# Decoder trunk on one core: residual kept by token, output, query and key products with the tokens as the stationary operand

## The chip, the cores and the metric

One core of one Trainium2 chip runs the whole program. The time is the device time of one execution in microseconds (us); the runs of the kernel before lie between 2883.8 and 2883.99.

## The reference

A trunk of two layers works on 256 tokens of 2048 features in float32. Each layer adds three branches to the residual `h`; all its weights are read once per execution.

```python
def reference(x, mem, ...):                      # D_MODEL 2048, SEQ 256, N_MEM 256, D_FF 5632, DEPTH 2
    h = x
    for l in range(DEPTH):
        h = h + hybrid_mixer(rms_norm(h, norm_mix[l]), ..., w_in[l], ..., w_out[l])
        h = h + memory_cross_attention(rms_norm(h, norm_x[l]), rms_norm(mem, norm_mem[l]),
                                       xa_wq[l], xa_wk[l], xa_wv[l], xa_wo[l])
        h = h + conv_ffn(rms_norm(h, norm_ffn[l]), ffn_w_up[l], ffn_conv[l], ffn_conv_b[l], ffn_w_down[l])
    return rms_norm(h, norm_final)

def memory_cross_attention(h, m, wq, wk, wv, wo):   # 4 heads of 512
    q, k, v = (h @ wq), (m @ wk), (m @ wv)          # each split into heads
    p = softmax(einsum('bthd,bmhd->bhtm', q, k) * 512 ** -0.5)
    return einsum('bhtm,bmhd->bthd', p, v) @ wo

def conv_ffn(h, w_up, conv_w, conv_b, w_down):
    g, val = split(causal_dwconv(h @ w_up, conv_w) + conv_b)   # 3 taps along the tokens
    return (silu(g) * val) @ w_down
```

The mixer projects into 4880 columns (linear attention, windowed attention, short convolution) and back with `w_out`.

## The kernel before

**Products.** Every float32 operand is split into a high and a low part (`hi = round(x)`, `lo = x - hi`), and a product is `hi*hi + hi*lo + lo*hi`. Weights come through `stream`: SyncE's queue (SP) loads a tile `raw` of 128 x 1024 (512 KB, 4 buffers), ScalarE (ACT) casts `wh` (line 160), VectorE (DVE) subtracts `wl` (line 161), with 3 buffers each. Two ways of multiplying stand side by side, and both sum in one of two pairs of PSUM banks:

- `wstat` keeps a 128 x 128 block of weights stationary. The result has features on partitions and tokens along the free axis. Its moving operand is the activations: `wh` meets 512 columns (high and low parts of 256 tokens), `wl` meets 256 columns (high parts). A group makes 256 features.
- `xstat` keeps 128 tokens stationary and moves the weights, 512 columns at a time. The result has tokens on partitions. A group makes 512 features.

In this text a **k step** is the work on 128 rows of a weight matrix and 512 of its columns. It takes 8 matmuls in `wstat` (four pairs of 512 and 256 columns) and 6 in `xstat` (all of 512 columns): 3072 columns either way. One `raw` tile holds two k steps.

**Layouts.** Before the change the residual `h` has features on partitions (8 tiles of 2 x 256). `w_fm` (part of the mixer's input), the keys `wk`, the queries `wq`, and the three products back to the residual, `wo`, `wxo` and layer 0's `wd` (tile `res`, `project_residual`), use `wstat`. `wv` (tile `vp`), `w_q`, `w_tok`, the feed-forward `wu` (tile `up`) and layer 1's last product `fin` keep tokens stationary. `up` has to be turned to features on partitions for the convolution: `turn` transposes 32 x 32 blocks on VectorE (line 226), writes the tile to DRAM (`z_d`, line 228, SP) and reads it back with the blocks in place (four DMAs, line 230, SP, which wait for the write). 44 groups of `up` are turned so. `ffn_group` then multiplies the turned tile by the row factors (line 1022).

**Residual.** After each of the eight groups of `res`, VectorE adds it to `h` in two instructions (lines 777 and 778), ScalarE squares it, VectorE sums the squares in `acc`, and `prep` makes the next stage's operand (lines 263 on ScalarE, 264 on VectorE) in place. `row_factor` sums `acc` over partitions with small matmuls (line 314, tile `ss`), takes the inverse root and spreads it over the partitions (line 299, tile `rbp`). In layer 1, `residual_by_token` turns `h` with 32 TensorE transposes (line 792, tile `hT`) during `up`, because `final` needs it by token.

**Order.** The program is written as one main line of products with tasks beside it (generators). Each call of `pump` lets one task run to its next `yield n`, after which it rests `n` calls. A product calls `pump` once or twice per k step, 32 times for 512 features in either form. `W` holds the rests: a turned group's second half waits `up=22` calls. A scheduler orders instructions on each engine from that program; `high_priority` moves some forward, `keep_in_program_order` holds some in place. Each engine and the SP queue run their instructions in order.

**Stages of a layer**, in order: `tokp`, `zkq`, `zq`, `zc`, `zb`, `zr` (mixer input), `kp` (keys), `res` from `wo`, `qp` (queries, with attention scores), `vp` (values), `res` from `wxo`, `up`, then `res` from `wd` (layer 0) or `fin` (layer 1).

Of the kernel before, what the change touches and what calls it, by code (L numbers as in the profile page):

```python
# [17 lines left out]
P = 128  # L18
D = 2048
# [32 lines left out]
         ms0=4, ms=8, xq=4, xp=8, xv=1, row=9, hT=9, up=22, up1=3, ss1=20, ss=9)  # L52
# [20 lines left out]
class Trunk:  # L73
# [110 lines left out]
    def xstat(self, xs, wd, gc=512, name="mm"):  # L184
# [3 lines left out]
        for k, wh, wl in self.stream(wd, gc, KT):  # L188
            x = xs(k // 2) if callable(xs) else xs[k // 2]
            for tb in range(2):  # L190
                ts = slice(tb * P, (tb + 1) * P)
                xh, xl = x[:, k % 2, 0, ts], x[:, k % 2, 1, ts]
                nc.tensor.matmul(ps[:, tb, :gc], lhsT=xh, rhs=wh, start=(k == 0), stop=False)  # L193
                nc.tensor.matmul(ps[:, tb, :gc], lhsT=xh, rhs=wl, start=False, stop=False)  # L194
                nc.tensor.matmul(ps[:, tb, :gc], lhsT=xl, rhs=wh, start=False, stop=(k == KT - 1))  # L195
                self.pump()
# [19 lines left out]
    def turn(self, ps, name="z"):  # L216
# [7 lines left out]
        with self.tc.high_priority(offset=WPRIO):  # L224
            for tb in range(2):
                nc.vector.transpose(out=zt[:, :, tb].rearrange("p b k i -> p k b i"),
                                    in_=ps[:, tb, :].rearrange("p (k b i) -> p k b i", k=4, b=4))
# [4 lines left out]
        return zf, zt.rearrange("p b t k i -> p (b t k i)").rearrange("p (k t) -> p k t", k=4)  # L232

# [34 lines left out]
    def squares(self, src, j, acc):  # L268

        nc = self.nc  # L270
        n = src.shape[1]
        sq = self.scratch("sq", (P, 2, T))
        nc.scalar.activation(sq[:, 0:n], src, AF.Square)
        if j == 0:
            nc.vector.tensor_tensor(acc[:, 0, :], sq[:, 0, :], sq[:, 1, :], ALU.add)
        else:
            for i in range(n):
                nc.vector.tensor_tensor(acc[:, 0, :], acc[:, 0, :], sq[:, i, :], ALU.add)
# [22 lines left out]
    def row_factor(self, acc, name, wait=1, *after):  # L301

        rc = self.rb.tile([P, 2], F32, tag=name + "c", name=name + "c")
        rbc = self.rb.tile([P, T], F32, tag=name + "b", name=name + "b")
        return rc, rbc, self.start(self._row_factor(acc, rc, rbc, wait), *after, first=True)

    def _row_factor(self, acc, rc, rbc, wait):
        nc = self.nc
        yield wait
        pss = self.bank("ss")  # L310
        for tb in range(2):
            n = acc.shape[1]
            for i in range(n):
                nc.tensor.matmul(pss[:, tb:tb + 1], lhsT=acc[:, i, tb * P:(tb + 1) * P], rhs=self.ones,
                                 start=(i == 0), stop=(i == n - 1))
        with self.tc.high_priority(offset=WPRIO):
            self.rsqrt_cols(pss[:, 0:2], 2, 1.0 / D, rc)
        yield W["row"]
        psb = self.bank("rbp")
        for tb in range(2):  # L320
            self.spread(psb[:, tb * P:(tb + 1) * P], rc[:, tb:tb + 1])
        nc.scalar.copy(rbc, psb[:, 0:T])

    def new_acc(self):
        return self.rb.tile([P, 2, T], F32, tag="acc", name="acc", bufs=1)


    def load(self):
# [15 lines left out]
        self.hp = [self.const.tile([P, 4, T], F32, name=f"h{c}") for c in range(4)]  # L344
        self.h = [self.hp[j // 2][:, 2 * (j % 2):2 * (j % 2) + 2, :] for j in range(8)]
        xs = {}

        def first(j):
            if j not in xs:
                nc.sync.dma_start(self.h[j], a["x"][j])  # L350
                xs[j] = self.prep(self.h[j], gm, j, self.operand("xs"))
# [9 lines left out]
        rc = self.rb.tile([P, 2], F32, tag="rxc", name="rxc")  # L361
        rbc = self.rb.tile([P, T], F32, tag="rxb", name="rxb")

        def factor():
            yield 9
            rest()
            yield from self._factor(a["xt"], rc, rbc, 2, 3)

        return first, (rc, rbc, factor())
# [315 lines left out]
    def mixer(self, l, xs, acc):  # L685
        nc, a = self.nc, self.a
        tok = [self.big(f"tok{tb}", [P, 2 * TOKC]) for tb in range(2)]
        if l == 0:
            rc, rbc, rt = acc
            rt = self.start(rt)  # L690
        else:
            rc, rbc, rt = self.row_factor(acc, "rx", W["ss1"])
# [34 lines left out]
        if l == 0:  # L727
            self.start(self.memory_factor())
# [39 lines left out]
    def project_residual(self, xs, w, gcol, kt=KT):  # L768

        nc = self.nc  # L770
        acc = self.new_acc()[:, 0:1, :]
        nxt = []
        for j in range(8):
            ps, h = self.wstat(xs, w[j], kt=kt, name="res"), self.h[j]
            if callable(gcol):
                gcol = gcol()
            nc.vector.tensor_tensor(h, ps[:, :, 0:T], h, ALU.add)
            nc.vector.tensor_tensor(h, ps[:, :, T:2 * T], h, ALU.add)
            self.squares(h, j, acc)
            nxt.append(self.prep(h, gcol, j, self.operand("xs")))  # L780
        return nxt, acc


    def residual_by_token(self):

        nc = self.nc
        for c in range(4):
            h = self.hp[c]
            pt = [self.bank("hT", (P, 4, P)) for _ in range(2)]
            for tb in range(2):  # L790
                for i in range(4):
                    nc.tensor.transpose(out=pt[tb][:, i, :], in_=h[:, i, tb * P:(tb + 1) * P], identity=self.ident)
                yield W["hT"]
            hv = h.rearrange("p (b a) t -> p b (a t)", b=2)
            for tb in range(2):
# [351 lines left out]
```

## Time and profile before

| What | Value |
|---|---|
| Median of 3 runs | 2883.9 us (2883.8 to 2883.99) |
| Profiled execution | 2891.09 us |
| Span of its instructions | 2889.3 us |
| TensorE matmul (PE) busy | 2865.4 us, 99% of the span |
| VectorE, ScalarE busy | 1904.0 us (66%), 1458.5 us (50%) |
| DMA | 579.39 MB, mean 201 GB/s |

PE is busy nearly all the time, but a busy PE is not a PE at its peak: a matmul's recorded duration overlaps the next one's. How fast a stage runs is read from the time between matmul starts and from the length of its stretch.

### The profile page before, as it was taken

The page shows a single profiled execution, that of the slowest core. Times are in us where ns is not written, and L with a number is a line of the kernel's source. Part 1 is how long each engine was busy: PE and PEld are TensorE (multiplying, and loading weights), DVE is VectorE, ACT ScalarE, POOL GpSimd, SP SyncE. Part 2 cuts the span into 40 slices and gives each one's busy share as a digit, 9 for nine tenths or more (in the row PEclk, how much of TensorE's full clock was granted, in tenths as well). Part 3 has the DMA queues.
Part 4 walks back from the last instruction along what each step waited for, and adds up shares of the span by engine and source line. Part 5 has one row for each costly group of instructions (what it writes and reads, how often), then busy time and mean ns, then how long its engine had stood idle before and what let it go on. Part 6 is the DMA issues. An engine that isn't in the chain of part 4 may idle for free.

```text
span 2889.3 us, 39601 instructions
## 1 busy us (share of the span) xinstructions
PE 2865.4 (99%) x14990; PEld 2435.6 (84%) x14990; DVE 1904.0 (66%) x2855; ACT 1458.5 (50%) x2034; POOL 15.8 (1%) x44
## 2 busy tenths in 40 slices
PE   9999999999999999999999999999999999999998
PEld 8888888888888888888888888888888878888886
DVE  6786665556677777755567866655567777776445
ACT  6565444445455555544455654444445555555333
POOL 0000000000000000000000000000000000000001
PEclk9999999999999999999999999999999999999999
DMA  7556655556777777766664566655567777777665
GB/s 240 157 174 204 186 187 168 168 167 185 226 240 240 240 247 236 241 186 189 183 179 143 165 197 186 187 161 168 174 185 224 237 235 242 237 242 247 197 194 156
DMA packets 181120, 579.39 MB, mean 201 GB/s; under 512 B 20640, under 2 KB 43712, under 8 KB 180928
## 3 DMA queue, kind: packets, MB, share of 16 engines
q1 hardware_dynamic: 180928, 576.85, 64.7%
q8 instruction: 117, 1.92, 0.3%
q14 instruction: 75, 0.61, 0.1%
HBM read 551.61 MB, written 25.17 MB: 200 GB/s over the span
## 4 chain that ended last, share of the span: by engine, by line
PE 80%; DMA 8%; DVE 8%; issue 2%; SPq 1%; ACT 1%; DVEq 0%; ACTq 0%
PE res L176 13%; PE fin L815 8%; PE res L177 7%; PE up L194 6%; PE up L195 6%; PE up L193 6%; DMA z_d<-z_t 4%; PE kp L176 4%; PE qp L176 4%; DMA z<-z_d 3%; DVE wl L161 3%; PE vp L195 2%; PE vp L194 2%; PE vp L193 2%; PE kp L177 2%
## 5 line engine op out<-in xcount | busy, mean ns | idle before, releaser
L161 DVE TENSOR_TENSOR wl<-raw,wh 128x1024 fp32r<-128x1024 f32 (+1 forms) x992 | 1201.8, 1212 | 755.8 <-ACT wh L160 754.0
L160 ACT CAST wh<-raw 128x1024 fp32r<-128x1024 f32 (+1 forms) x992 | 1034.4, 1044 | 1090.9 <-PE up L195 322.9
L194 PE MATMUL up<-wl,xs 128*128 128x512 f32 x1408 | 550.2, 391 | 3.3 <-DVE wl L161 2.9
L195 PE MATMUL up<-wh,xs 128*128 128x512 f32 x1408 | 548.3, 389 | 0.0
L193 PE MATMUL up<-wh,xs 128*128 128x512 f32 x1408 | 548.3, 389 | 0.0
L194 PEld LDWEIGHTS up<-wl,xs 128*128 128x128 f32 x1408 | 264.3, 188 | 63.1 <-DVE wl L161 8.3
L193 PEld LDWEIGHTS up<-wh,xs 128*128 128x128 f32 x1408 | 264.3, 188 | 54.7
L195 PEld LDWEIGHTS up<-wh,xs 128*128 128x128 f32 x1408 | 264.3, 188 | 54.2
L176 PE MATMUL res<-a,wh 128*128 128x512 f32 x688 | 241.1, 395 | 0.0
L177 PE MATMUL res<-a,wl 128*128 128x256 f32 x688 | 192.9, 280 | 0.0
L815 PE MATMUL fin<-wh,a 128*128 128x512 f32 x704 | 189.9, 389 | 0.0
L176 PE MATMUL qp<-xs,wh 128*128 128x512 f32 x480 | 171.6, 397 | 0.0
L176 PE MATMUL res<-xo,wh 128*128 128x512 f32 x480 | 170.5, 398 | 0.0
L176 PE MATMUL kp<-ms,wh 128*128 128x512 f32 x480 | 169.5, 397 | 0.0
L815 PEld LDWEIGHTS fin<-wh,a 128*128 128x128 f32 x704 | 132.1, 188 | 27.4
L176 PEld LDWEIGHTS res<-a,wh 128*128 128x128 f32 x688 | 129.0, 187 | 29.9
L177 PE MATMUL res<-xo,wl 128*128 128x256 f32 x480 | 135.0, 281 | 0.0
L177 PE MATMUL qp<-xs,wl 128*128 128x256 f32 x480 | 134.9, 281 | 0.0
L177 PE MATMUL kp<-ms,wl 128*128 128x256 f32 x480 | 134.6, 280 | 0.0
L177 PEld LDWEIGHTS res<-a,wl 128*128 128x128 f32 x688 | 130.0, 189 | 0.4
L995 ACT ACTIVATE u<-z_t,par 128x256 f32<-128x256 f32 x176 | 91.6, 591 | 59.8 <-DVE z_t L1022 59.7
L815 PE MATMUL fin<-wl,a 128*128 128x512 f32 x352 | 110.0, 389 | 0.0
(332 smaller groups left out, 4274.0 us busy)
## 6 DMA issues: line engine op xcount, KB each, us to landing
raw<-in_wu SPq DMA_DIRECT2D x352, 512.0 KB, 4.6
raw<-in_wd SPq DMA_DIRECT2D x176, 512.0 KB, 4.2
raw<-in_w_fm SPq DMA_DIRECT2D x80, 512.0 KB, 4.5
raw<-in_wk SPq DMA_DIRECT2D x64, 512.0 KB, 4.7
raw<-in_wo SPq DMA_DIRECT2D x64, 512.0 KB, 4.6
raw<-in_wq SPq DMA_DIRECT2D x64, 512.0 KB, 4.5
raw<-in_wv SPq DMA_DIRECT2D x64, 512.0 KB, 3.6
raw<-in_wxo SPq DMA_DIRECT2D x64, 512.0 KB, 4.5
```

Of the source, the lines that this page charges most:

```text
L160: nc.scalar.copy(wh[:, :n], raw[:, :n])
L161: nc.vector.tensor_tensor(wl[:, :n], raw[:, :n], wh.bitcast(F32)[:, :n], ALU.subtract)
L176: nc.tensor.matmul(ps[:, m, :], lhsT=wh[:, ms], rhs=xhl, start=(k == 0), stop=False)
L177: nc.tensor.matmul(ps[:, m, 0:T], lhsT=wl[:, ms], rhs=xh, start=False, stop=False)
L193: nc.tensor.matmul(ps[:, tb, :gc], lhsT=xh, rhs=wh, start=(k == 0), stop=False)
L194: nc.tensor.matmul(ps[:, tb, :gc], lhsT=xh, rhs=wl, start=False, stop=False)
L195: nc.tensor.matmul(ps[:, tb, :gc], lhsT=xl, rhs=wh, start=False, stop=(k == KT - 1))
L815: nc.tensor.matmul(ps[c][tb], lhsT=lhs, rhs=w[v][:, c % 2 * 512:c % 2 * 512 + 512], start=(k == 0 and n == 0), stop=(k == FT - 1 and n == 2))
L995: nc.scalar.activation(u[:, s, :], z[:, s, :], AF.Identity, bias=self.p[:, C_FB + m:C_FB + m + 1], scale=tap[2])
```

## The change

The residual is kept by token in four tiles `h[c]` of 2 x 512. `kp`, `qp` and the three kinds of `res` use `xstat` in groups of 512 features: four groups for each where there were eight. Their weights are laid out in DRAM for 512 columns; bytes read are the same.

`project_residual` adds a group to `h[c]` on VectorE, turns it through DRAM as `up` is turned, squares it on ScalarE with a running sum, and starts `next_operands`, which after 24 calls of `pump` makes two operand tiles from the turned copy (four ScalarE and eight VectorE instructions with strided views). The next stage's product asks for its operands as it needs them (`when`). Keys and queries are turned the same way (`cross_key`, `cross_query`), 22 calls later. That makes 36 turned groups more: 8 of keys, 8 of queries, 20 of `res`.

`row_factor` reduces the running sums on VectorE instead of multiplying on TensorE, and for the cross-attention no factor is spread. `residual_by_token` is gone. At the start, `x` by features goes to scratch tiles, and `x` by token is loaded into `h` directly (it went through the `raw` buffers before, for the sum of squares alone).

```diff
-    def turn(self, ps, name="z"):
+    def turn(self, src, name="z"):
...
-    def squares(self, src, j, acc):
...
+    def squares(self, c, ss):
+        for tb in range(2):
+            self.nc.scalar.activation(self.scratch("sq"), self.h[c][:, tb], AF.Square,
+                                      accum_out=ss[:, 4 * tb + c:4 * tb + c + 1])
...
     def _row_factor(...):
-        pss = self.bank("ss")
-                nc.tensor.matmul(pss[:, tb:tb + 1], lhsT=acc[:, i, tb * P:(tb + 1) * P], rhs=self.ones, ...)
+            nc.vector.tensor_reduce(sm, ss.rearrange("p (b c) -> p b c", b=2), AX.X, ALU.add)
+            self.rsqrt_cols(sm, 2, 1.0 / D, rc)
+        if rbc is not None:
...
     def load(self):
-                nc.sync.dma_start(self.h[j], a["x"][j])
-                xs[j] = self.prep(self.h[j], gm, j, self.operand("xs"))
+                xf = self.t512("xf", (P, 2, T))
+                nc.sync.dma_start(xf, a["x"][j])
+                xs[j] = self.prep(xf, gm, j, self.operand("xs"))
...
+            for c in range(4):
+                nc.sync.dma_start(self.h[c], a["xt"][c])
+                yield 2
+                self.squares(c, ss)
+                yield 2
...
     def project_residual(self, xs, w, gcol, kt=KT):
-        for j in range(8):
-            ps, h = self.wstat(xs, w[j], kt=kt, name="res"), self.h[j]
+        for c in range(4):
+            ps, h = self.xstat(xs, w[c], kt=kt, name="res"), self.h[c]
...
-            nc.vector.tensor_tensor(h, ps[:, :, 0:T], h, ALU.add)
-            nc.vector.tensor_tensor(h, ps[:, :, T:2 * T], h, ALU.add)
-            self.squares(h, j, acc)
-            nxt.append(self.prep(h, gcol, j, self.operand("xs")))
-        return nxt, acc
+            with self.tc.high_priority(offset=WPRIO):
+                for tb in range(2):
+                    nc.vector.tensor_tensor(h[:, tb], ps[:, tb], h[:, tb], ALU.add)
+            zf, _ = self.turn(h, "hf")
+            self.squares(c, ss)
+            ts.append(self.start(self.next_operands(c, zf, gcol, nxt), first=True))
+        return self.when(ts, nxt, 2), ss
...
-    def residual_by_token(self):
...
+    def next_operands(self, c, zf, gcol, out):
+        nc = self.nc
+        yield W["nx"]
+        for j in range(2):
+            x = self.operand("xs")
+            for i in range(2):
+                k = 2 * j + i
+                g = gcol[:, 4 * c + k:4 * c + k + 1]
+                src = zf[:, :, :, k, :]
+                hi, lo = (x[:, i, u, :].rearrange("p (b a i) -> p a b i", b=2, a=4) for u in range(2))
+                self.tc.keep_in_program_order(nc.scalar.activation(hi, src, AF.Copy, scale=g))
+                for tb in range(2):
+                    self.tc.keep_in_program_order(nc.vector.scalar_tensor_tensor(
+                        lo[:, :, tb], src[:, :, tb], g, hi.bitcast(F32)[:, :, tb], ALU.mult, ALU.subtract))
+            out.append(x)
+            yield 1
...
     def cross_keys(self, l, ms):
-        for g in range(8):
-            z = self.fold(self.wstat(ms, self.a["wk"][l, g], name="kp"))
-            self.by_row(z, self.mrbc)
-            ks.append(self.operand_of(z, f"k{g}"))
+        ts = [self.start(self.cross_key(self.turn(self.xstat(ms, self.a["wk"][l, hd], name="kp")), ks[hd]), self.tm)
+              for hd in range(4)]
...
     def cross(self, l, xs, ss, ms, ks):
-            for g in range(2):
-                z = self.fold(self.wstat(xs, a["wq"][l, 2 * hd + g], name="qp"))
-                qs.append(self.operand_of(z, "q"))
+            tq = self.start(self.cross_query(self.turn(self.xstat(xs, a["wq"][l, hd], name="qp")), qs))
```

What stands in a row on three engines, at the places that matter most:

TensorE, at the beginning of layer 0's product with `wo`. Before (`oc` are activations; the operand named first is the moving one):

```order
L179 MATMUL kp<-ms_2607,wl 128x256
L180 MATMUL kp<-ms_2607,wh 128x512
L176 MATMUL res<-oc_1499,wh 128x512
L177 MATMUL res<-oc_1499,wl 128x256
L176 MATMUL res<-oc_1499,wh 128x512
```

TensorE, the same place in the changed kernel:

```order
L194 MATMUL kp<-wl,ms_2623 128x512
L195 MATMUL kp<-wh,ms_2623 128x512
L193 MATMUL res<-wh,oc_1513 128x512
L194 MATMUL res<-wl,oc_1513 128x512
L195 MATMUL res<-wh,oc_1513 128x512
```

The pairs of 512 and 256 columns (eight matmuls per k step) have become runs of three of 512 (six per k step).

VectorE, around the end of the last group of the same product, where the queries' product follows. Before:

```order
L161 TENSOR_TENSOR wl<-raw,wh 128x1024 x2
L777 TENSOR_TENSOR h_116<-res,h_116 128x512
L778 TENSOR_TENSOR h_116<-res,h_116 128x512
L161 TENSOR_TENSOR wl<-raw,wh 128x1024
L278 TENSOR_TENSOR acc<-acc,sq 128x256
L264 SCALAR_TENSOR_TENSOR xs<-h_116,par,xs 128x256
L278 TENSOR_TENSOR acc<-acc,sq 128x256
L264 SCALAR_TENSOR_TENSOR xs<-h_116,par,xs 128x256
L161 TENSOR_TENSOR wl<-raw,wh 128x1024 x2
```

VectorE, the same place in the changed kernel (`hf_t` is the transposed copy of `h`):

```order
L799 SCALAR_TENSOR_TENSOR xs<-hf,par,xs 128x128 x8
L161 TENSOR_TENSOR wl<-raw,wh 128x1024 x3
L781 TENSOR_TENSOR h_116<-res,h_116 128x512 x2
L226 STREAM_TRANSPOSE hf_t<-h_116 128x4x4x32
L161 TENSOR_TENSOR wl<-raw,wh 128x1024
L226 STREAM_TRANSPOSE hf_t<-h_116 128x4x4x32
```

The add is followed by the two transposes, with a weight tile between them, and no operand is made there.

VectorE, some rows later in the changed kernel, in the first group of the queries' product (`hf` is the copy read back, `z_t` the transposed group of queries):

```order
L161 TENSOR_TENSOR wl<-raw,wh 128x1024 x2
L799 SCALAR_TENSOR_TENSOR xs<-hf,par,xs 128x128 x8
L161 TENSOR_TENSOR wl<-raw,wh 128x1024 x3
L226 STREAM_TRANSPOSE z_t<-qp 128x4x4x32 x2
L161 TENSOR_TENSOR wl<-raw,wh 128x1024 x4
```

The operands that were made at once, from `h`, now come four weight tiles after the transposes, behind two DMAs and ahead of the stage's next weights.

SP's queue at the same place in the changed kernel (before, there are 32 loads of `wo` and then 32 of `wq` with nothing between):

```order
L230 DMA hf<-hf_d 32x4x256 x4
L158 DMA raw<-in_wq 128x1024 x7
L228 DMA hf_d<-hf_t 128x1024
L158 DMA raw<-in_wq 128x1024
L230 DMA hf<-hf_d 32x4x256 x4
L158 DMA raw<-in_wq 128x1024 x6
```

The write of the transposed tile stands behind seven weight loads of the next stage, and one more load stands between it and the four reads.

## Rows read from the trace of the kernel before

**Rows 1.** The page: busy shares, and granted clock in 40 slices.

```profile
PE 2865.4 (99%) x14990; PEld 2435.6 (84%) x14990; DVE 1904.0 (66%) x2855; ACT 1458.5 (50%) x2034; POOL 15.8 (1%) x44
...
PEclk9999999999999999999999999999999999999999
```

**Rows 2.** Stages: tokp, res of wo, up, res of wd, tokp, up, fin.

```profile
core 0: us, PE busy (x) PEld busy (x) DVE busy (x) ACT busy (x) POOL busy (x), PEclk, DMA share, GB/s
6.10:46.40 40.30, 36.52 (x197) 34.44 (x198) 28.88 (x74) 27.28 (x46) 0.00 (x0) 1.00 0.90 304
334.00:424.40 90.40, 90.40 (x513) 78.54 (x512) 59.76 (x76) 44.11 (x55) 0.00 (x0) 1.00 0.60 187
717.60:1199.90 482.30, 480.73 (x2122) 397.02 (x2122) 357.62 (x529) 257.80 (x349) 0.00 (x0) 1.00 0.75 237
1199.90:1446.30 246.40, 246.40 (x1410) 215.43 (x1409) 133.71 (x147) 104.87 (x117) 3.15 (x6) 1.00 0.65 193
1446.30:1481.50 35.20, 35.20 (x201) 35.20 (x200) 20.22 (x36) 16.23 (x21) 0.00 (x0) 1.00 0.66 188
2150.70:2638.00 487.30, 485.60 (x2149) 398.99 (x2148) 359.25 (x533) 259.72 (x353) 0.00 (x0) 1.00 0.75 236
2638.00:2877.50 239.50, 239.50 (x1057) 198.01 (x1055) 119.77 (x125) 98.12 (x106) 4.62 (x4) 1.00 0.65 190
```

**Rows 3.** Timeline, PE, product with wd: start us, us, instruction.

```profile
1209.76 0.40 PE L176 MATMUL res<-a,wh 128*128 128x512 f32 x1
1209.99 0.28 PE L177 MATMUL res<-a,wl 128*128 128x256 f32 x1
1210.11 0.40 PE L176 MATMUL res<-a,wh 128*128 128x512 f32 x1
```

**Rows 4.** Timeline, PE, in up of layer 1.

```profile
2329.66 0.39 PE L194 MATMUL up<-wl,xs 128*128 128x512 f32 x1
2329.89 0.39 PE L195 MATMUL up<-wh,xs 128*128 128x512 f32 x1
2330.11 0.39 PE L193 MATMUL up<-wh,xs 128*128 128x512 f32 x1
2330.34 0.39 PE L194 MATMUL up<-wl,xs 128*128 128x512 f32 x1
```

**Rows 5.** Groups: line engine op out<-in xcount | busy us, mean ns | idle before.

```profile
L792 PE MATMUL hT<-con,h 128*128 128x128 f32 x32 | 5.8, 273 | 0.0
L299 PE MATMUL rbp<-con,rxc 128*128 128x128 f32 x20 | 3.2, 274 | 0.0
```

**Rows 6.** Tile ss on PE: duration ns min/median/max, first and last start.

```profile
L314 PE MATMUL ss<-ones,acc x20: 164/250/250, 431.8 to 2159.2; 128*128 128x1 f32 x20
```

**Rows 7.** Groups of ScalarE and VectorE, columns as in Rows 5.

```profile
L161 DVE TENSOR_TENSOR wl<-raw,wh 128x1024 fp32r<-128x1024 f32 (+1 forms) x992 | 1201.8, 1212 | 755.8 <-ACT wh L160 754.0
L226 DVE STREAM_TRANSPOSE z_t<-up 128x512 f32<-128x512 f32 x88 | 57.5, 691 | 2.6 <-PE up L195 1.8
L777 DVE TENSOR_TENSOR h<-res,h 128x512 f32<-128x512 f32 x40 | 27.6, 691 | 30.0 <-PE res L180 30.0
L264 DVE SCALAR_TENSOR_TENSOR xs<-h,par,xs 128x256 fp32r<-128x256 f32 x80 | 37.5, 478 | 0.0
L263 ACT ACTIVATE xs<-h,par 128x256 fp32r<-128x256 f32 x80 | 35.8, 495 | 0.7 <-PE res L177 0.7
```

**Rows 8.** Chain in order of time: three turns in up, write and read.

```profile
763.71 4.44 DMA z_d<-z_t
769.49 4.28 DMA z<-z_d
829.83 4.81 DMA z_d<-z_t
835.98 5.02 DMA z<-z_d
2331.97 7.27 DMA z_d<-z_t
2340.58 3.21 DMA z<-z_d
```

**Rows 9.** Line 228, the write to DRAM, issue to landing.

```profile
L228 SPq DMA_DIRECT2D z_d<-z_t x44: 326/327/331, 742.0 to 2640.5; - x44
...
DMA to landing us min/median/max: 3.1/4.8/7.3
```

**Rows 10.** Line 230, each read back, issue to landing.

```profile
L230 SPq DMA_DIRECT2D z<-z_d x176: 303/428/2017, 745.7 to 2646.7; - x176
...
DMA to landing us min/median/max: 2.4/3.0/5.1
```

**Rows 11.** What PE waited for: us in total, times, longest us.

```profile
PE tokp L211 <- ACT wh L160: 3.3, 2, 2.3
PE up L194 <- DVE wl L161: 2.9, 5, 0.9
```

More of the change, by code (lines that the diff above doesn't have):

```diff
@@ L232, in turn, with turned_by_row, when, operand @@
         return zf, zt.rearrange("p b t k i -> p (b t k i)").rearrange("p (k t) -> p k t", k=4)
+    def turned_by_row(self, z, zf, rbc):
+        for tb in range(2):
+            ts = slice(tb * P, (tb + 1) * P)
+            self.tc.keep_in_program_order(self.nc.vector.tensor_tensor(
+                z[:, :, ts].rearrange("p k (a i) -> p k a i", a=4), zf[:, :, tb].rearrange("p a k i -> p k a i"),
+                rbc[:, ts].rearrange("p (a i) -> p a i", a=4).unsqueeze(1).broadcast_to([P, 4, 4, 32]), ALU.mult))
+    def when(self, ts, out, n):
+        def operand(j):
+            self.until(ts[j // n])
+            return out[j]
+        return operand
     def fold(self, ps, name="z", z=None):
@@ L299, in spread, with row_factor, _row_factor @@
         self.nc.tensor.matmul(ps, lhsT=col.broadcast_to([P, P]), rhs=self.ident, start=True, stop=True)
-    def row_factor(self, acc, name, wait=1, *after):
+    def row_factor(self, ss, name, wait=1, after=(), row=True):
         rc = self.rb.tile([P, 2], F32, tag=name + "c", name=name + "c")
-        rbc = self.rb.tile([P, T], F32, tag=name + "b", name=name + "b")
-        return rc, rbc, self.start(self._row_factor(acc, rc, rbc, wait), *after, first=True)
-    def _row_factor(self, acc, rc, rbc, wait):
+        rbc = self.rb.tile([P, T], F32, tag=name + "b", name=name + "b") if row else None
+        return rc, rbc, self.start(self._row_factor(ss, rc, rbc, wait), *after, first=True)
+    def _row_factor(self, ss, rc, rbc, wait):
         nc = self.nc
         yield wait
-        pss = self.bank("ss")
[L311 to L315, printed above, removed]
-        with self.tc.high_priority(offset=WPRIO):
[L317 to L325, printed above, removed]
+        sm = self.cols("sm", 2)
+        with self.tc.high_priority(offset=WPRIO):
+            nc.vector.tensor_reduce(sm, ss.rearrange("p (b c) -> p b c", b=2), AX.X, ALU.add)
+            self.rsqrt_cols(sm, 2, 1.0 / D, rc)
+        if rbc is not None:
+            yield W["row"]
+            psb = self.bank("rbp")
+            for tb in range(2):
+                self.spread(psb[:, tb * P:(tb + 1) * P], rc[:, tb:tb + 1])
+            nc.scalar.copy(rbc, psb[:, 0:T])
     def load(self):
@@ L682, in swa, with mixer @@
             self.split(out[i][:, :, 0, ts], out[i][:, :, 1, ts], ov[:, 2 * i:2 * i + 2, :])
-    def mixer(self, l, xs, acc):
+    def mixer(self, l, xs, ss, after):
         nc, a = self.nc, self.a
         tok = [self.big(f"tok{tb}", [P, 2 * TOKC]) for tb in range(2)]
[L688 to L692, printed above, removed]
+        rc, rbc, rt = self.row_factor(ss, "rx", W["ss1"] if l else 1, after)
         pst = self.xstat_both(xs, a["w_tok"][l], name="tokp")
@@ L781, in project_residual @@
-        return nxt, acc
-    def residual_by_token(self):
-        nc = self.nc
[L787 to L795, printed above, removed]
-                (nc.vector.tensor_copy if tb else nc.scalar.copy)(hv[:, tb], pt[tb].rearrange("p i t -> p (i t)"))
-            yield W["hT"]
+            with self.tc.high_priority(offset=WPRIO):
+                for tb in range(2):
+                    nc.vector.tensor_tensor(h[:, tb], ps[:, tb], h[:, tb], ALU.add)
@@ L835, in finish @@
         nc = self.nc
[L836 removed]
+        hv = [h[:, tb] for h in self.h]
         for c, h in enumerate(hv):
@@ L952, in cross_values, with cross @@
             self.split(out[e2][:, :, 0, :], out[e2][:, :, 1, :], po)
-    def cross(self, l, xs, acc, ms, ks):
+    def cross(self, l, xs, ss, ms, ks):
         nc, a = self.nc, self.a
-        rc, _, rt = self.row_factor(acc, "rx", W["ss"])
+        rc, _, rt = self.row_factor(ss, "rx", W["ss"], row=False)
         sc = None
```

123 lines of the change are left out of this document (59 added, 64 removed).

## Prediction

> **What bounds the kernel now.** I read the page first: TensorE's matmul row is busy 99% of the span, VectorE 66%, ScalarE 50%, and the granted clock is in its top tenth in all 40 slices [rows 1]; in each stretch that I opened it is 1.00, the upper of its two levels, 2.4 GHz [rows 2]. The table of waits says the same in another way: the two longest waits of TensorE that concern us add up to 6 us, 3.3 at the start and 2.9 in up [rows 11]. So the span is TensorE's issue rate, stage after stage, and the change has to be costed as time per k step, not as busy time. The stretches give it [rows 2]. The product with wo is 64 k steps in 90.4 us, 1.4125 us each. The product with wd is 176 in 246.4, 1.400. Both are the form with weights stationary. up of layer 0 is 352 k steps in 482.3 us, 1.370, up of layer 1 is 352 in 487.3, 1.384, and fin is 176 in 239.5, 1.361. These three have the tokens stationary. The timeline shows why they differ although the columns are the same: a pair of 512 and 256 columns starts 0.35 us after the pair before it [rows 3], four pairs 1.40; three matmuls of 512 start within 0.68 us [rows 4], six 1.36.
>
> **Products moved to tokens stationary.** Keys, queries, wo and wxo are 128 k steps each over both layers, wd of layer 0 is 176: 688 in all. The new form's price needs a choice. fin (1.361) has no turn beside it, up has one turn every 16 k steps like the changed stages, with the same DMA load on top of the weights (237 GB/s against 187 in wo [rows 2]) and even more work on VectorE. I take up of layer 0, 1.370. The four products with 128 k steps then give 512 x (1.4125 - 1.370) = 21.8 us, all four counted at wo's price because their forms are wo's. wd gives 176 x (1.400 - 1.370) = 5.3 us. Together **27.1 us**, all of it on the path, since TensorE does not wait there now. At fin's price it would be 33.2 us, at that of up of layer 1 (1.384, which also carries most of the hT transposes) 17.4 us. These are the ends.
>
> A page speaks against that term: the Trainium skill, "TensorE: Matmul & The Clock Gate", section "Back-to-back issue gap", has the gap of an isolated matmul as its columns at 2.4 GHz plus about 2.5 ns, so equal columns cost nearly equal time. Worked out from that figure (an estimate), 8 matmuls against 6 differ by 5 ns per k step, and the 688 would give 3.4 us. The rows differ by more than 40 ns per k step [rows 2 to 4], and the sum goes by them.
>
> **TensorE work that disappears.** 32 hT transposes, recorded as 5.8 us; the up that carries most of them is 5.0 us longer than the other [rows 2, 5]. 20 products for ss at 0.25 us recorded, and 8 of the 20 rbp at 0.274 (four for each of the five factors, and the two of the cross-attention are no longer spread) [rows 5, 6]. As recorded that is 5.8 + 5.0 + 2.2 = 13.0 us, but recorded durations overlap: the rows have 0.39 us where matmuls start 0.227 apart [rows 4], a ratio of 0.58, which gives 7.5. A product with one column streams next to nothing, so I take **5 us**, with 3 and 10 as ends.
>
> **VectorE and ScalarE.** Half the evictions and all adds to acc go, two transposes per group come (0.69 us each [rows 7]). Both engines have time free in these stages (59.8 and 44.1 of 90.4 us busy in wo [rows 2]). I cost this at nothing: TensorE's next product hides it, as two pairs of PSUM banks stand ready. What matters is only where one of them waits with weight tiles queued behind it.
>
> **The new wait: the way through DRAM.** Call the first matmul of the group after a res group zero. VectorE adds twice, transposes, makes one weight tile, transposes: 2 x 0.691 + 0.691 + 1.212 + 0.691 = 4.0 us [rows 7]. On SP the write stands behind seven weight loads; the last of them needs the raw buffer that this same weight tile frees, so the write leaves at about 4.0. From its issue to the last landing the chain shows 10.1, 11.2 and 11.8 us for three turns of up (763.71 to 773.77, 829.83 to 841.00, 2331.97 to 2343.79 [rows 8]); the chain holds the late ones, and the medians give 4.8 for the write, three more issues of 0.43 and 3.0 for a read, 9.1 us [rows 9, 10]. So the turned tile is there at 13.1 in the middle and 15.8 at the late end. With the first ScalarE instruction (0.495 [rows 7]) the next stage's operand 6 is begun at 13.6 to 16.3. TensorE comes to it after 12 k steps of 1.36 us, at 16.3. Nothing is lost in the middle, and nothing much at the late end. It is needed so early in four places only, wo to queries and wxo to up in each layer. From wd to tokp a k step is 35.2 / 16 = 2.2 us [rows 2] and the turn has 26 us.
>
> What queues behind the waiting VectorE is the weight tile for k steps 14 and 15, in all 20 res groups. The eight operand instructions have half the width of line 264's 0.478 us [rows 7]; I take 0.35 us each, 2.8. The tile is ready at 13.1 + 0.5 + 2.8 + 1.2 = 17.6 us in the middle, 20.3 at the late end; TensorE's second matmul of k step 14 starts at 14 x 1.36 + 0.23 = 19.3. So a late turn costs up to 1.0 us, a usual one nothing. SP's weight loads behind the four reads are held until about 10 us; the next of them is for the following group, needed at 21.8. Scores wait for turned queries, but stand on TensorE more than 10 k steps into the next group (13.6 us), about when an undelayed turn without adds is through (two transposes and 9.1 us, 10.5); late, up to 13.2. I take **1 us** lost over all of this beyond what the price of up holds already, with 0 and 10 as ends.
>
> **The start.** tokp takes 40.3 us in layer 0 and 35.2 in layer 1 [rows 2]; the 5.1 us are waits for loads, 3.3 of them on ScalarE's cast [rows 11]. The change brings the four loads of x by token forward and keeps them out of the raw buffers: the same bytes, some weights later, then fewer blocked. Bounds from this row: 3 us either way. I take 0.
>
> **Sum.** 27.1 + 5 - 1 = 31.1 us. The profiled execution, 2891.09 us with a span of 2889.3, would become 2860; it lies 7.2 us above the median of the runs, so the median 2883.9 becomes **2853 us**, 1.1% faster.
>
> **Rivals.** (a) The turns cost more than in up of layer 0: price 1.384 and 1 us at each of the four early places. 17.4 + 5 - 4 = 18.4 us, 2865.5. For it: the second up is slower with the same work. Against: much of that is hT, and the changed stages have less work on VectorE. (b) Equal columns cost equal time, the lower price of up being due to something else in that stage, such as its operands. Only the 5 us stay: 2879, within 0.2%. This is what the page cited above would make of it. Against: fin and up, with different operands, agree to 0.01 us, and so do wo and wd in the other form. (c) **Slower**: the turn becomes the bound. In each of the 20 res groups VectorE stands before the turned tile and the weight tile behind it is late. By the times above the loss per group is the time from write to last landing less 10.8 us; it eats the gain of 32.1 us where it is 1.6 us per group, so from a mean of 12.4 us. At 14 us it is 3.2 x 20 = 64, and the time 2916. For it: the longest write and the longest read are 7.3 and 5.1 [rows 9, 10], 13.7 with the issues. Against: no turn in the chain shows more than 11.8 us. (d) The start loses or gains 3 us: inside the range.
>
> **How the numbers follow.** Forecast 0.72, (a) 0.16, (b) 0.05, (c) 0.05, the rest 0.02. Faster by over 0.2% (which is about what a measurement of this kernel can tell from no change; below 2878) is forecast and (a) and half the rest, 0.89; within it (b) and a little, 0.06; slower (c), 0.05. The range: the forecast's own ends are 33.2 + 10 + 3 and 17.4 + 3 - 10, not all at once; I take gains of 15 to 38 us, 2846 to 2869, which holds (a) and leaves out (b) and (c).
>
> **What would show it.** After: wo in 87 to 88 us, wd in about 241, up of layer 1 within 1 us of layer 0; three matmuls within 0.68 us in res, kp and qp; about 1400 fewer matmuls; granted clock 1.00 throughout; TensorE's waits for wl under 8 us in all, none over 2 us after a res group. It is wrong if TensorE waits on next_operands' instructions or on wl for more than 1 us in most groups, if res runs at 1.40 per k step, or if writing and reading back take over 12 us in the res stages.

## The result and the profile after

| | Before | After |
|---|---|---|
| Median | 2883.85 us (2883.54 to 2883.99, 4 runs) | 2845.55 us (2844.15 to 2846.51, 4 runs) |
| Profiled execution, its span | 2891.09, 2889.3 us | 2846.51, 2844.7 us |

The ratio is 0.9867 [0.985, 0.9884]: 38.3 us faster, where 31 were forecast. The direction is as predicted; the time lies 7.5 us under the forecast and just below the range's low end of 2846.

The page of the kernel after, the rows that answer to [rows 1]:

```profile
PE 2825.5 (99%) x13554; PEld 2363.4 (83%) x13554; DVE 1885.5 (66%) x2877; ACT 1445.7 (51%) x2060; POOL 15.8 (1%) x44
...
PEclk9999999999999999999999999999999999999999
```

TensorE is as full as before, with 1436 matmuls fewer. So again the stretches have to be read. Stage table of the kernel after: keys of layer 0, wo, up, wd, then tokp, up and fin of layer 1 (columns as in [rows 2]):

```profile
243.80:330.60 86.80, 86.80 (x384) 71.85 (x383) 52.41 (x54) 38.49 (x41) 0.00 (x0) 1.00 0.75 233
330.60:417.60 87.00, 87.00 (x385) 72.06 (x384) 56.28 (x74) 43.06 (x58) 0.00 (x0) 1.00 0.74 240
704.20:1183.80 479.60, 479.60 (x2118) 396.90 (x2118) 360.06 (x536) 259.46 (x354) 0.00 (x0) 1.00 0.75 241
1183.80:1423.10 239.30, 239.30 (x1057) 198.18 (x1056) 127.94 (x142) 104.20 (x120) 3.14 (x6) 1.00 0.69 211
1423.10:1458.00 34.90, 34.90 (x198) 34.86 (x197) 21.96 (x43) 17.67 (x27) 0.00 (x0) 1.00 0.77 221
2114.20:2593.40 479.20, 479.20 (x2117) 396.85 (x2116) 361.65 (x537) 259.26 (x354) 0.00 (x0) 1.00 0.76 244
2593.40:2832.90 239.50, 239.50 (x1057) 198.01 (x1055) 118.80 (x124) 98.13 (x106) 4.63 (x4) 1.00 0.64 188
```

wd takes 239.3 us, as long as fin beside it: 1.360 us per k step in both. wo is at 87.0 / 64 = 1.359, keys at 86.8 / 64 = 1.356 (the first of their 384 matmuls ran ahead of the stretch; with it 1.360). Both stretches of up are shorter than in [rows 2] too, although their products were not changed, and both are now within 0.4 us of each other.

TensorE's waits in the kernel after (us in total, times, longest):

```profile
PE zkq L177 <- DVE wl L161: 2.5, 2, 1.3
PE tokp L211 <- DVE wl L161: 1.5, 4, 0.9
PE tokp L211 <- ACT wh L160: 1.4, 2, 1.2
PE cold L346 <- DVE cold L343: 1.1, 1, 1.1
PE tokp L211 <- ACT xs L278: 0.5, 1, 0.5
```

This is the whole list. There is no wait in res, kp, qp or up: the way through DRAM has left nothing on TensorE.

Timeline of TensorE in wd of the kernel after, against [rows 3]:

```profile
1300.06 0.39 PE L193 MATMUL res<-wh,a 128*128 128x512 f32 x1
1300.28 0.39 PE L194 MATMUL res<-wl,a 128*128 128x512 f32 x1
1300.51 0.39 PE L195 MATMUL res<-wh,a 128*128 128x512 f32 x1
1300.73 0.39 PE L193 MATMUL res<-wh,a 128*128 128x512 f32 x1
```

Three matmuls start within 0.67 us, as up's did in [rows 4].

### The profile page after: what moved, and what is told of

Same layout as the page of the kernel before. It is cut to its first block, busy times and chain, and to the rows that moved or that the text cites. A ratio compares the mean times of both kernels' runs of the same rounds, so it can differ in the third digit from the quotient of the medians.

```text
span 2844.7 us, 37041 instructions
## 1 busy us (share of the span) xinstructions
PE 2825.5 (99%) x13554; PEld 2363.4 (83%) x13554; DVE 1885.5 (66%) x2877; ACT 1445.7 (51%) x2060; POOL 15.8 (1%) x44
## 4 chain that ended last, share of the span: by engine, by line
PE 98%; DVE 1%; DMA 1%; ACT 0%; issue 0%; SPq 0%; ACTq 0%
PE up L194 11%; PE up L195 11%; PE up L193 11%; PE fin L821 8%; PE res L195 7%; PE res L193 7%; PE res L194 7%; PE qp L194 2%; PE vp L193 2%; PE vp L195 2%; PE vp L194 2%; PE qp L193 2%; PE qp L195 2%; PE kp L195 2%; PE kp L193 2%; PE kp L194 2%
## 5 line engine op out<-in xcount | busy, mean ns | idle before, releaser
L193 PE MATMUL res<-wh,a 128*128 128x512 f32 x352 | 136.9, 389 | 0.0
L194 PE MATMUL res<-wl,a 128*128 128x512 f32 x352 | 136.9, 389 | 0.0
L195 PE MATMUL res<-wh,a 128*128 128x512 f32 x352 | 136.9, 389 | 0.0
L193 PE MATMUL vp<-wh,ms 128*128 128x512 f32 x256 | 100.3, 392 | 0.0
L193 PE MATMUL qp<-wh,xs 128*128 128x512 f32 x256 | 100.2, 391 | 0.0
L194 PE MATMUL qp<-wl,xs 128*128 128x512 f32 x256 | 100.0, 391 | 0.0
L195 PE MATMUL vp<-wh,ms 128*128 128x512 f32 x256 | 99.9, 390 | 0.0
L194 PE MATMUL vp<-wl,ms 128*128 128x512 f32 x256 | 99.8, 390 | 0.0
L195 PE MATMUL qp<-wh,xs 128*128 128x512 f32 x256 | 99.8, 390 | 0.0
L193 PE MATMUL res<-wh,xo 128*128 128x512 f32 x256 | 99.6, 389 | 0.0
```

## The experiments

**Theory 1**: the new form runs at fin's price, six matmuls 0.227 us apart, and not at that of up of layer 0; what up gained is the work taken off TensorE and waits that the profiled execution of before happened to hold; the turns cost nothing. Its rivals stand in the expectations.

### The kernel before, profiled again (no edit)

> The kernel before, profiled a second time, to see whether the waits for wl in up and its 1.370 and 1.384 us per k step belong to the kernel or to that one execution. Theory 1, they belonged to the execution (its 2891.09 us lie 7.2 above the median of the unprofiled runs): up of layer 0 takes 479 to 480 us as in the changed kernel, TensorE's waits for wl in up are under 1 us, and the execution is within 2 us of 2884. Theory 2, they belong to the kernel: up takes 482 and 487 us again with about 3 us of waits, and the execution is near 2891.

Measured (one execution): 2884.45 us, span 2882.7, that is 6.6 us less than the profiled execution of before. Stage table of this execution, up of layer 0 and of layer 1:

```profile
715.60:1195.40 479.80, 479.80 (x2122) 397.33 (x2122) 360.10 (x530) 257.95 (x349) 0.00 (x0) 1.00 0.75 238
...
2146.30:2631.40 485.10, 484.07 (x2150) 399.55 (x2149) 360.21 (x533) 259.67 (x353) 0.00 (x0) 1.00 0.75 237
```

And its waits in up:

```profile
PE up L194 <- DVE wl L161: 1.0, 2, 0.8
```

up of layer 0 is 2.5 us shorter than in [rows 2], up of layer 1 2.2 us, with 1.0 us of waits where [rows 11] have 2.9, and the two waits are both in layer 1. So 482.3 was not the price of that stage. Undisturbed it is 479.8 / 352 = 1.363 us per k step, fin's price within 0.2%.

### The kernel after, profiled again (no edit)

> The changed kernel once more, as the base of the next two runs on their chip. Theory 1 (the products' new price and the work taken off TensorE make the time, and nothing of a turn is left on the path): 2845 to 2847 us, wo 87.0, layer 0's wd 239.3, both stretches of up within 0.5 us of 479.4, and no wait of TensorE in up or in the products back to the residual. If the absence of waits was a piece of luck of the one execution looked at, waits of 1 to 5 us for wl show in up or after groups of res.

Measured: 2845.52 us (2844.43 to 2846.3), ratio 0.9866 [0.985, 0.9883], span of the profiled execution 2843.3; wo 87.04, wd 239.36, both stretches of up 479.20, and again no wait outside tokp and zkq. So the account can be made between executions with few waits, from the first matmul of one stage to the first of the next (us):

| Stretch | before, second execution | after | after, second execution |
|---|---|---|---|
| tokp, layer 0 | 40.14 | 41.62 | 40.68 |
| keys, both layers | 179.54 | 173.66 | 173.67 |
| wo, both layers | 180.80 | 174.16 | 174.13 |
| queries, values, wxo, both layers | 586.56 | 573.22 | 573.22 |
| wd | 246.40 | 239.35 | 239.36 |
| **sum of these four** | **1193.30** | **1160.39** | **1160.38** |
| up, layer 0 | 479.72 | 479.53 | 479.20 |
| tokp, layer 1 | 35.28 | 34.83 | 34.83 |
| up, layer 1 | 485.12 | 479.20 | 479.20 |
| span | 2882.7 | 2844.7 | 2843.3 |

Of 38.0 us between the spans of the first two columns, 32.9 are in the four stretches of the changed products (values and scores, which lie in them, kept their form), 5.9 in up of layer 1 (1.0 of it waits), 0.6 in the other up and tokp, and the start gives back 1.5. Nothing is left over beyond 0.1.

The stretches hold small matmuls too. Added over the trace from each matmul's start to the next one's, keys, queries, wo, wxo and wd together take 968.8 us in the second execution of before and 937.1 in the first of after, 31.7 less. Of the 32.9, some 1.8 are small matmuls beside the queries and wxo, eight of ss and eight of rbp among them, and the values' products took 0.6 more.

Nor are the waits in up those of one execution. In two further runs with the old residual (keys alone and split keys, below), up of layer 0 took 480.8 and 482.0 us with 0.4 and 1.1 us of waits, and up of layer 1 took 483.1 in both, without a wait. With keys alone, layer 1:

```profile
2143.50:2626.60 483.10, 483.10 (x2149) 399.83 (x2148) 363.32 (x534) 259.78 (x353) 0.00 (x0) 1.00 0.75 239
```

So some 3.9 of the 5.9 us are work taken off, and 2.0 are the waits and what they delayed; the table of waits has 1.0.

### Keys alone

```diff
-    z = self.fold(self.wstat(ms, self.a["wk"][l, g], name="kp"))
-    self.by_row(z, self.mrbc)
+    self.cross_key(self.turn(self.xstat(ms, self.a["wk"][l, hd], name="kp")), ...)
```

> Only the keys go to tokens stationary with a turn through DRAM; residual, queries and transposes stay. Theory 1, the price of the new form is 1.360 us per k step with nothing lost to the turns: the two stretches of kp go from 89.8 to 86.8 us, 6 us in all, 2878. Theory 2, each turn costs what I put into the forecast's price or more: 5 us or less, 2879 to 2882. A rule by which equal columns cost equal time gives 2883.

Measured: 2877.76 us against 2884.92 for before beside it, ratio 0.9976 [0.9966, 0.9985]. Stage table, keys of both layers:

```profile
244.30:331.20 86.90, 86.90 (x385) 71.91 (x385) 52.51 (x54) 38.59 (x41) 0.00 (x0) 1.00 0.74 232
1672.90:1759.80 86.90, 86.90 (x385) 71.91 (x385) 52.51 (x54) 38.63 (x41) 0.00 (x0) 1.00 0.76 232
```

The turned keys without any turned residual run as in the full change: 89.8 to 86.9 in each layer. That the gain belongs to the keys' new form itself, with its turns, is shown.

### Residual products alone

The kernel after, with keys and queries taken back to `wstat`, groups of 256 and no turn.

```diff
-    ... self.turn(self.xstat(xs, a["wq"][l, hd], name="qp")) ...
+    z = self.fold(self.wstat(xs, a["wq"][l, 2 * hd + g], name="qp"))
```

Keys are taken back in the same way.

> The changed kernel with keys and queries back to weights stationary, so that the residual by token with its 20 turned groups stands alone. Theory 1: wo, wxo and wd give 3.4 us for each 90 us stretch and 7.1 for wd, 20.5 in all, and 5 us of small TensorE work goes, 2858. Theory 2, by the forecast's price of 1.370: 10.9 + 5.3 + 5 = 21.2, 2862.7.

Measured: 2859.42 us (2858.09 to 2863.16), ratio 0.9915 [0.99, 0.993]; wo is 87.1 and wd 239.3. Its gain of 25.5 and the keys' 7.2 leave 5.6 of the 38.3 us for the queries, whose products take 180.8 us before and 175.3 after, start to start: about additive. The only wait for a turned tile in all versions with the full rest of 24 calls shows here:

```profile
PE qp L176 <- ACT xs L797: 2.4, 2, 1.3
```

A group of 256 features goes through its operands in half the time, so queries in the old form reach the last turned operands sooner. That this is the reason is argued, not tried.

### The same columns in more matmuls

Keys of the kernel before, with each matmul of 512 columns split into two of 256 on the same stationary block, in 14 of the 16 k steps of each group (the first and the last keep the old form). The arithmetic is unchanged. Cut to the lines that change:

```diff
-    nc.tensor.matmul(ps[:, m, :], lhsT=wh[:, ms], rhs=xhl, ...)
+    nc.tensor.matmul(ps[:, m, 0:T], lhsT=wh[:, ms], rhs=xh, ...)
+    nc.tensor.matmul(ps[:, m, T:2 * T], lhsT=wh[:, ms], rhs=x[:, k % 2, 1, :], ...)
```

> The kernel before with the product for the keys as three matmuls of 256 columns where it had one of 512 and one of 256, 12 matmuls per k step and not 8, the same columns (14 of 16 k steps of each group). It asks what the old form loses: theory A, a fixed cost of some 13 ns for each matmul (0.2267 us for 512 columns at 2.4 GHz is 0.2133 and 0.0134): 12 x 0.120 = 1.44 us per k step, a kp stretch of about 92 us for 89.8. Theory B, a narrow matmul does not cover the load of the next weights, and it is the load that shows (the pair's 0.352 us is 0.117 and 0.235): 0.125 us or more for each, 1.50 or more, 95 us or more.

Measured (one execution): 2887.28 us against 2883.42 for before beside it. Stage table, keys of both layers, then TensorE's timeline there:

```profile
241.70:333.30 91.60, 91.60 (x737) 90.18 (x736) 54.87 (x57) 42.95 (x49) 0.00 (x0) 1.00 0.60 189
1676.10:1767.70 91.60, 91.60 (x737) 90.18 (x736) 54.87 (x57) 42.94 (x49) 0.00 (x0) 1.00 0.61 189
```

```profile
279.79 0.28 PE L176 MATMUL kp<-ms,wh 128*128 128x256 f32 x1
279.91 0.28 PE L177 MATMUL kp<-ms,wh 128*128 128x256 f32 x1
280.03 0.28 PE L178 MATMUL kp<-ms,wl 128*128 128x256 f32 x1
280.15 0.28 PE L176 MATMUL kp<-ms,wh 128*128 128x256 f32 x1
```

The same 3072 columns per k step take 1.431 us in this run (twelve matmuls in 14 of 16 k steps), 1.403 in eight, 1.356 in six. Starts are 0.120 us apart at 256 columns and 0.227 at 512 (medians over these stages), at 2.4 GHz 13 ns above the columns in either case: theory A. Equal columns do not cost equal time: the number of matmuls counts. In the old form a pair of 512 and 256 took 0.350 us in wd and 0.353 in wo, 3 to 6 ns more than 0.227 + 0.120. So of the 40 (wd) to 53 ns (wo) saved per k step some 26 are the two matmuls. The rest is left to the alternation of widths; that is argued, and why wo pays more for it than wd is open.

### A shorter rest before the operands

```diff
-    nx=24
+    nx=16
```

> The changed kernel with the operands of the next stage placed 16 calls behind the turn and not 24, 4 k steps (5.4 us) earlier in the order of ScalarE and VectorE; no work changes. Theory 1, the way through DRAM takes 13 to 14 us from the group's end and is hidden only because its readers stand behind 12 k steps of weights: the operands end near 16.5 us, the weight tile for k steps 10 and 11 follows at 17.7 where TensorE wants it at 13.8, so up to 3.9 us in each of 20 groups, 78 us, 2880 to 2924, with TensorE waiting for wl in res and after it. Theory 2, the turn is too short or the buffers too deep for this to matter: within 4 us of 2845.5.

Measured (one execution): 2869.89 us, 24 more than the kernel after, wo 92.0, no change in up. The direction is Theory 1's, the size below what it gave. TensorE's waits:

```profile
PE res L194 <- DVE wl L161: 10.8, 15, 0.8
PE res L193 <- ACT wh L160: 2.7, 4, 1.1
```

VectorE's timeline after the first group of wd, kernel after, up to the tile behind the operands (adds, transposes, weight tiles, operands; in brackets the idle time before and its releaser):

```profile
1243.82 1.29 DVE L781 TENSOR_TENSOR h<-res,h 128x512 f32<-128x512 f32 x2 [0.41 <-PE res L195]
...
1255.78 1.23 DVE L161 TENSOR_TENSOR wl<-raw,wh 128x1024 fp32r<-128x1024 f32 x1 [1.49 <-ACT wh L160]
1257.50 2.20 DVE L799 SCALAR_TENSOR_TENSOR xs<-hf,par,xs 128x128 fp32r<-128x128 f32 x8 [0.49 <-ACT xs L797]
1259.64 1.23 DVE L161 TENSOR_TENSOR wl<-raw,wh 128x1024 fp32r<-128x1024 f32 x1
```

The same place with 16 calls:

```profile
1252.82 1.29 DVE L781 TENSOR_TENSOR h<-res,h 128x512 f32<-128x512 f32 x2 [0.41 <-PE res L195]
...
1262.06 1.23 DVE L161 TENSOR_TENSOR wl<-raw,wh 128x1024 fp32r<-128x1024 f32 x1 [1.45 <-ACT wh L160]
1266.53 2.19 DVE L799 SCALAR_TENSOR_TENSOR xs<-hf,par,xs 128x128 fp32r<-128x128 f32 x8 [3.24 <-ACT xs L797]
1268.67 3.49 DVE L161 TENSOR_TENSOR wl<-raw,wh 128x1024 fp32r<-128x1024 f32 x3
```

In both, the operands come 13.7 us after the adds, since they wait for the turned tile. But with 16 calls four weight tiles stand ahead of them, with 24 five. Eight calls fewer moved the operands by one weight tile (2.7 us), not by the four k steps (5.4 us) that Theory 1 had counted; VectorE's order is the scheduler's. The tile behind them is then the one for k step 12 and not 14. With 16 calls it is ready 16.9 to 19.2 us after the adds begin, 17.7 in the mean, and TensorE, whose next group begins 0.2 us before the adds, comes to it at 12 x 1.36 + 0.23 - 0.2 = 16.35. That is 1.36 us late in each of the 19 groups that the product or a next stage with short k steps follows, 26 us; 24 were measured.

### A longer rest

```diff
-    nx=24
+    nx=28
```

> The changed kernel with the rest before the next stage's operands at 28 calls of pump in place of 24. In VectorE's order the eight operand instructions then stand behind six weight tiles after most groups of res where there were five, 2.7 us later. Theory 1: with five tiles the weight tile behind them is ready before TensorE comes to it, so one more gives nothing: within 2 us of the changed kernel's time. Rival, that TensorE still loses time after the turns in a form that the table of waits does not show, as with 16 calls (four tiles) but smaller: shorter by 5 us or more, wo below 86.5.

Measured (one execution): 2846.54 us, wo 87.05, wd 239.36, up 479.20 twice. No gain: with five tiles the cover is enough, and no loss hides that the table of waits would not show.

### The transposes put back

The kernel after, with the 32 TensorE transposes of the residual and eight copies during up of layer 1; their results are not used.

```diff
+    nc.tensor.transpose(out=pt[tb][:, i, :], in_=h[:, tb, i * P:(i + 1) * P], identity=self.ident)
+    (nc.vector.tensor_copy if tb else nc.scalar.copy)(self.t512("hd"), pt[tb]...)
```

> The changed kernel with the 32 transposes of the residual put back into up of layer 1, with their copies out of PSUM into scratch; their result is not used. Theory 1, they cost what TensorE issues for them, 2.4 to 5 us: 2848 to 2850.5. Theory 2, their copies also delay weight tiles, as up of layer 1 of the kernel before suggests: 6 us or more, 2852 or more, with waits for wl in up.

Measured: 2850.01 us (2848.33 to 2851.42), 4.5 above the kernel after. Stage table, up of layer 1:

```profile
2115.70:2597.80 482.10, 482.10 (x2141) 399.04 (x2140) 364.70 (x540) 260.52 (x357) 0.00 (x0) 1.00 0.76 242
```

It is 2.9 us longer, and wxo ahead of it, where the first transposes fell, 0.9: 3.8 us for 32 transposes recorded as 8.7 (0.272 each), 0.12 each. No wait for a weight tile appears in up, so the second theory falls.

### The mixer's products turned too

If turning costs nothing and every k step in the old form costs 0.04 to 0.05 us more, `zc`, `zb` and `zr` (64 k steps per layer) should give up to 6 us.

```diff
-    z = fm(4 + j, "zc")
+    self.turned_conv(j, self.turn(self.xstat(xs, a["w_fm"][l, 1 + j], name="zc")), rbc, ys)
```

`zb` and `zr` are turned alike.

> The changed kernel with three more parts of the mixer's input (convolution, its gate, the linear attention's gate; 128 k steps over both layers) moved to tokens stationary and turned, 8 turned groups more. Theory 1, the gain is the issue rate and the turn is hidden wherever the result is needed a group later: 128 x 0.046 = 5.9 us less than the changed kernel's 2845.5, 2839.7. Theory 2, the gain comes with the residual's layout and not with the form: no change, 2845; or a wait appears in the attention stages, where small products share TensorE, and it is slower.

Measured: 2848.97 us (2847.23 to 2849.51), no gain. From the first matmul of `zc` to the last of the keys, with the turned mixer and without:

```profile
132.60:332.60 200.00, 196.49 (x894) 160.57 (x893) 142.58 (x249) 107.68 (x179) 0.65 (x8) 1.00 0.71 224
1546.40:1741.40 195.00, 194.31 (x889) 160.28 (x888) 140.87 (x235) 104.42 (x172) 0.65 (x8) 1.00 0.70 221
```

```profile
134.40:330.60 196.20, 196.20 (x1021) 167.25 (x1020) 142.62 (x250) 111.49 (x187) 0.65 (x8) 1.00 0.66 207
1544.70:1740.50 195.80, 195.80 (x1017) 166.76 (x1016) 141.60 (x236) 108.66 (x180) 0.65 (x8) 1.00 0.64 199
```

The matmuls themselves start 0.227 us apart in the middle, but TensorE now waits there, which it does not in the kernel after. VectorE, which has softmax and gates in this stage, stands 4.1 us before one turned tile of `zc` with weight tiles and softmax behind it:

```profile
173.74 1.29 DVE L238 TENSOR_TENSOR z_t<-z,rxb 128x512 f32<-128x512 f32 x2 [4.12 <-DMA z<-z_d]
```

The same with 30 calls of rest for these groups, where 22 were:

```diff
-    yield W["up"]
+    yield W["tm"]
```

> The kernel in which zc, zb and zr of the mixer's input are turned too, with 30 calls of pump before a turned group is used in place of 22. With 22 their products ran at the new price in the middle (three matmuls of 512 in 0.68 us), but TensorE lost 6.0 us to late weights, softmax sums and casts in layer 0's stretch and 1 to 2 in layer 1's. Theory A, these waits come from VectorE standing before the turned tile (4.1 us once, at 169.6): with 30 calls they go, the stretch from zc to the end of zr falls from 106.4 us per layer to about 104, and the time to 2841 to 2843. Theory B, VectorE has too much of its own work in this stage (softmax, gates) for a tile that comes late anyway: stretch 105 to 110, time 2845 to 2850, as with 22.

Measured: 2843.56 us (2843.0 to 2847.84), ratio 0.9862 [0.9848, 0.9877]. The same stretches, in the execution that took 2847.84:

```profile
134.70:329.60 194.90, 194.23 (x893) 160.91 (x892) 142.12 (x249) 107.47 (x179) 0.65 (x8) 1.00 0.72 229
1544.10:1741.90 197.80, 195.80 (x889) 161.42 (x888) 140.84 (x235) 104.32 (x172) 0.65 (x8) 0.99 0.70 218
```

Layer 0 has recovered from 200.0 to 194.9, so standing before the turned tile was a part of the loss. Layer 1 of this execution has waits of its own (one for a weight tile, 1.8 us), and behind that wait the granted clock was down, at the lower of its two levels (1.2 GHz):

```profile
1637.00:1640.00 3.00, 2.88 (x7) 2.30 (x8) 2.73 (x4) 0.00 (x0) 0.00 (x0) 0.50 0.81 287
```

Matmuls of 512 columns started 0.43 us apart there, which cost some 1.6 us more. Without the two, layer 1 would stand near 194.4, as layer 0 does. The other three executions took 2843.0 to 2843.9. The median is 2.0 us below the kernel after beside it, with overlapping intervals: between the two expectations, and no version that can be called better. A part of the 6 us was never there: start to start, `zc` and `zb` took 88.8 and 44.6 us over both layers in this execution, 90.3 and 45.5 in the old form, and 1.360 per k step would be 87.0 and 43.5. Among the small matmuls of attention the new form does not reach its price; why is open.

## Why the prediction missed its range

**The price of the new form is the step that failed.** Of the two prices in [rows 2] I took that of up of layer 0, 1.370, because it has turns as the changed stages have. The changed products saved 31.7 us where that price gives 27.1; fin's 1.361, named as the upper end, gives 33.2. up's 482.3 us held waits, in part listed in [rows 11] as 2.9 us over both layers, 1.5 of them in that stretch. I read that row and then used the stretch as if it were issue rate alone. The second execution, without a wait in that stretch, has 1.363, and at that price the term is 31.9. The reason given for the choice, the turns beside the products, has no cost that shows: start to start, keys, wo, wxo and wd run at 1.360 to 1.361 with turns beside them. Queries alone stand at 1.370, with the small matmuls of the scores between them; that these are the reason is not tried. All four products at wo's price is a small fault in the other direction: keys had 180.0 / 128 = 1.406 and not 1.4125, 0.8 us in all.

**Work taken off TensorE** was forecast at 5 us (3 to 10) and gave about 6.3: 3.9 in up of layer 1, 1.8 beside the queries and wxo, 0.6 in the other up and tokp. The transposes alone gave 3.8 when put back. That scaling their 5.8 us by the ratio of start spacing to duration comes near (3.4) is luck: the ratio belongs to single durations, 32 x 0.273 = 8.7 us, and gives 5.0; the 5.8 of [rows 5] has overlaps counted once already.

**The way through DRAM** was forecast at 1 us and cost nothing. Its arithmetic held: in the 19 groups that short k steps follow, the weight tile behind the operands is ready 17.2 to 19.2 us after TensorE's next group begins (17.6 in the middle forecast, 20.3 late) and is needed at 19.3. The margin is thin, 0.1 us at the worst group, and the run with 16 calls shows the loss when one weight tile of it is gone. The 20 turns of the residual took 9.3 to 11.3 us from the write's issue to the last landing (9.1 to 11.8 forecast). Line 228 of the kernel after, issue to landing (the last line is over all 80 writes of that line), against [rows 9]:

```profile
L228 SPq DMA_DIRECT2D hf_d<-hf_t x20: 326/327/620, 356.2 to 2118.1; - x20
...
DMA to landing us min/median/max: 2.7/4.7/5.6
```

36 more turned groups and 240 GB/s in wo (187 in [rows 2]) made the write no slower.

**The start**, forecast at 0 with 3 us either way, gave 0.5 to 1.5 us back between the executions of the table. Over all runs tokp of layer 0 takes 39.6 to 41.9 us with the old start and 39.9 to 42.6 with the new, so no gain or loss stands clear of the scatter; what part the clock has in the long ones with the new start is told at the end.

**Sum.** 31.7 for the products, 6.3 for the work taken off, 2.0 for the waits in up of layer 1, less 0.6 for the values and 1.5 for the start, is 37.9 us of the 38.0 between the spans; 27.1 + 5 - 1 + 0 was forecast. The price is 4.6 of the difference, the waits in up 2.0, the work 1.3, the way through DRAM 1; values and start go the other way. Setting the sum against the median was right: the profiled execution lay 7.2 us above it, and the second one lies at the median without that excess. But a price taken from a stretch of that execution carried a part of its excess into the sum.

**The rivals.** (a) and (c) fall with the list of waits; (c) lives in the run with 16 calls, at 1.2 us per group. (b), equal columns at equal time, is refuted by the split keys and by the stretches of the changed products. The Trainium skill, "TensorE: Matmul & The Clock Gate", section "Back-to-back issue gap", gives an isolated matmul 216 ns at 512 columns and, by its formula, 109 at 256 (an estimate); the starts here are 227 and 120 ns apart, 11 ns more in each. Its sustained 131 ns for 512 columns is seen in no row here.

**What would show it** came as listed, but for wd, 239.3 where 241 was named, and the clock, 1.00 except at one place of the start (below).

## What to carry over

Before a stretch serves as a price, take out the waits that the profile lists in it, or better, take an execution with none, since the 1.5 us listed in up of layer 0 made it 2.5 us longer: here the two candidates differed by 0.7% and the choice was worth 6 us. With TensorE the bound, count matmuls as well as columns: the same columns in six matmuls of one width in place of eight of two gave 3 to 4%. A round trip of 10 us cost nothing here as long as the instruction that waits for it stood behind enough of the weight tiles on its engine; count the cover in those tiles, in the scheduled order, and not in calls or k steps.

## What the hardware showed beside this

At a granted clock of 1.00 a matmul of these operands costs its columns at 2.4 GHz and 13 ns more, at 256 and 512 columns alike (0.120 us less 0.107, 0.227 less 0.213); where widths of 512 and 256 alternate a pair costs 3 to 6 ns more than that (0.350 to 0.353).

In the start of the first execution of the kernel after, the granted clock fell from the upper of its two levels (2.4 GHz) to the lower (1.2 GHz) for a part of two stretches. Stage table, stretches of tokp in that execution:

```profile
25.00:30.00 5.00, 2.90 (x13) 2.26 (x12) 4.51 (x19) 3.89 (x7) 0.00 (x0) 0.87 0.53 195
30.00:35.00 5.00, 5.00 (x24) 5.00 (x23) 4.80 (x25) 1.34 (x2) 0.00 (x0) 0.78 0.74 239
35.00:46.00 11.00, 11.00 (x65) 11.00 (x64) 5.95 (x10) 6.32 (x11) 0.00 (x0) 1.00 0.67 206
```

TensorE had been busy for 2.9 of the 5 us from 25 to 30, otherwise waiting for weights, and the clock stayed down into the next stretch, where it was busy throughout: 24 matmuls in 5 us. The second execution waited as long there (2.8 us busy of 5), kept 1.00 in both stretches and made 30 matmuls in the second. tokp was 0.9 us longer in the execution whose clock fell. It is no single case: of the eight profiled executions with the new start, five show the fall at this place (0.66 to 0.78 in the stretch from 30 to 35 us) and take 41.1 to 42.6 us in tokp of layer 0; the three that kept 1.00 (the second execution, 16 calls, the mixer with 22) take 39.9 to 40.7. All other stages shown above are at 1.00, but for the mixer's with 30 calls (0.99), where the clock fell once more behind a wait. What decides between the two is open.
